# Pacing the last head's sums, splitting two weight sums ahead, and moving one norm step in a two-layer decoder trunk

## The chip, the cores and the metric

The kernel runs on one core of a Trainium2 chip. The metric is the device time of one execution in microseconds (us), taken as the median of three runs. The engines are named as the profile names them: PE is TensorE's matmuls, PEld its weight loads, DVE is VectorE, ACT is ScalarE, POOL is GpSimd and SP is SyncE, which here only issues DMAs. "SPq" and "POOLq" are the DMA queues of SP and POOL.

## The reference

The reference is two layers on x of shape (1024 positions, 1024 channels), all in fp32:

```python
for i in range(2):
    if i == 0:  y = mlstm_branch(x)       # x @ w_in, conv, 4 heads of a chunked matrix memory, group norm, gates, @ w_out
    else:       y = shortconv_branch(x)   # x @ w_in (1024x8192), gated 3-tap conv, silu gate, @ w_out (2048x1024)
    x = layer_norm(ALPHA * x + y, ln_g[i], ln_b[i])
    gate = sigmoid(x @ ple_gate_w[i])
    x = x + gate * (p[i] @ ple_w[i])
```

## The kernel before, in words

All activations lie channels first: a tile is 128 channels by 512 positions ("a slot"; 98 slots rotate), and h = 0 or 1 is the half of the positions. One fp32 product is made of three matmuls (`three`, L101 to L106): each operand is split into a high part that is rounded to fp32r (a cast on ACT, L91) and a low part, the rest (a subtraction on DVE, L94; L128 and L129 for a negated operand). L104 is high by high, L105 low weights by high, L106 high by low: "PE waits for L94" means that a low part was late. The big products use Strassen-like sums, seven products in place of eight, so weights and moving tiles are first added to each other. DVE makes such sums of moving tiles (`combined`, L118); DMAs that add in memory make those of weights (`add_on`, L135, on POOL's queue).

The program is written out in order by Python. A scheduler keeps that order mostly, engine by engine; generators that are stepped between products decide where the small work stands. The stages, by their part names: "in" (first projection), "at" (the four heads; items of one 128-position key block each), "outa" (projection out of layer 0), "ga" (norm and gate of layer 0), "b" (first projection of layer 1 with its convolution), "outb" (projection out of layer 1), "gb" (norm and gate of layer 1, output).

What the change touches:

- `norm` (L850 to L912) is the group norm after a head's half. For each of four channel tiles c it transposes on PE (L573), and DVE multiplies by the weight and the gate (L891) and adds the skip (L893). When four tiles of a pair are there, they are stored to DRAM (`store_plain`), and `store_sums` (L158) makes four sums on DVE (L118) and stores them on SP's queue (L152). For heads 0 to 2 that is done in the norm; for the last head the sums are deferred to `finish_cell` (L1369), which makes four at once in every second unit of outa from unit 9 on. The last head's h = 1 norm runs beside the first units of outa.
- `Out` (L198) runs a projection out as 56 units, each one weight tile and one moving tile, 12 matmuls. `load` fetches them about four units ahead by SP (L227), `prepare` splits both two units ahead. The weights of units s1 to s4 are sums that `weight_sums` (L171) made earlier and kept in DRAM (`wsdram`) as one fp32 tile each. Each of `outa` and `outb` is one `Out`.
- `layer_norm` (L1021) runs as a generator beside the matmuls. It makes the mean by matmul (L1017 with `mean`), subtracts (DVE L1036), squares (ACT L1038), adds the squares on POOL (L1010, L1012), and gets the variance (L1047). Then a diagonal tile is made (L1057), split, and multiplied by ones (`rs`, L1017 with `onesr`), so that 1/sigma stands in every partition. After it DVE multiplies eight tiles by `rs` (L1069) and ACT scales each (L1070). `NORM_WAITS[h]` says how many steps lie between these. In ga the gate of h = 1 needs those eight tiles; the gate's groups for h = 0 run meanwhile, each ending in a sigmoid (ACT L1186), a product and a sum on DVE (L1187, L1188) and splits for layer 1 (L91, L128, L1405).

Of the kernel before, what the change touches and what calls it, by code (L numbers as in the profile page):

```python
# [60 lines left out]
def trunk(ctx: ExitStack, tc: tile.TileContext, I, out: bass.AP):  # L61
# [48 lines left out]
    ydram = dr.tile([2, 7, 8, P, HALF], F32, name="ydram")  # L110
    wsdram = dr.tile([2, 4, 8, P, HALF], F32, name="wsdram")
    gwdram = dr.tile([2, 4, 7, 2, P, HALF], F32, name="gwdram")
# [45 lines left out]
    def store_sums(layer, kk, y11, y12, y21, y22):  # L158
        n3 = combined(y12, y22, ALU.subtract)
        t1 = combined(y12, y11, ALU.subtract)  # L160
        t2 = combined(y11, n3, ALU.subtract)
        n4 = combined(y21, t2, ALU.subtract)
        for what, y in (("t2", t2), ("t1", t1), ("n3", n3), ("n4", n4)):
            store(layer, kk, what, y)

    def store_moving(layer, kk, *ys):

        store_plain(layer, kk, *ys)
        store_sums(layer, kk, *ys)

    def weight_sums(layer, weights):  # L171

        rows = lambda k, i: weights[cols(k), cols(i, HALF)]
        store = lambda n, kk, t: nc.sync.dma_start(wsdram[layer, n, kk], t)
        s4 = None
        for kk in range(8):
            if s4 is not None:
                store(3, kk - 1, s4)
            s1, s2, s3, s4 = (slot() for _ in range(4))
            for t, src in ((s1, rows(2 * kk, 1)), (s2, rows(2 * kk, 0)), (s3, rows(2 * kk, 0)),  # L180
                           (s4, rows(2 * kk + 1, 0))):
                nc.sync.dma_start(t, src)
            yield
            add_on(s1, rows(2 * kk + 1, 1))
            add_on(s3, rows(2 * kk, 1))
            yield
            add_on(s2, s1)
            store(0, kk, s1)
            store(2, kk, s3)
            s1 = s3 = None  # L190
            yield
            add_on(s4, s2)
            store(1, kk, s2)
            s2 = None
            yield
        store(3, 7, s4)

    class Out:  # L198
# [8 lines left out]
        def __init__(self, layer, weights, residual):  # L207
            self.w, self.y, self.x, self.ready = {}, {}, {}, {}
            self.loads, self.loaded, self.prepared = [], 0, 0
            rows = lambda k, i: weights[cols(k), cols(i, HALF)]  # L210
            for what, kk in self.UNITS:
                if what in SUMS:
                    w = wsdram[layer, SUMS.index(what), kk]
                else:
                    w = rows(2 * kk + (what != "a11"), int(what == "a22"))
                m = MOVING[what]
                unit = [(self.w, (what, kk), w), (self.y, (m, kk), ydram[layer, STORED.index(m), kk])]
                for c, h, when in ((0, 0, ("a12", 4)), (0, 1, ("s2", 4)), (4, 1, ("s3", 4)), (4, 0, ("a22", 4))):
                    if (what, kk) == when:
                        unit += [(self.x, (c + t, h), residual(c + t, h)) for t in range(4)]  # L220
                self.loads.append(unit)

        def load(self, n):
            while self.loaded < min(n, len(self.UNITS)):
                for dst, key, src in self.loads[self.loaded]:
                    dst[key] = slot()
                    nc.sync.dma_start(dst[key], src)  # L227
# [519 lines left out]
    outa = Out(0, I["woa"], lambda k, h: I["xt"][cols(k), cols(h, HALF)])  # L747
    sums = weight_sums(0, I["woa"])

# [100 lines left out]
    def norm(hd, h, num, pacc, mv):  # L850
# [101 lines left out]
    for i in range(len(cell.order)):  # L952
# [11 lines left out]
        if i > 40 and cell.order[i][1] in (2, 5):  # L964
            step(sums)
        if i >= last:
            planned(i - last - 8)
# [5 lines left out]
    for _ in range(LEADS):  # L973
        lead()
    side = iter(())
    for i, (hd, h, s) in enumerate(items):
# [13 lines left out]
        if s >= 4 * h:  # L990
            close(num, s - 4 * h, mv)
        for _ in range(2):
            step(side)
        if i % 2:
            step(sums)
        outa.load((i - len(items) + 10) // 2)
        outa.prepare((i - len(items) + 6) // 2)
        if s == 4 * h + 3:
            drain(side)
            side = norm(hd, h, num, state.pop((hd, h))[1], mv)  # L1000
    last_norm = side
    drain(sums)
# [16 lines left out]

    NORM_WAITS = ((1, 3, 8, 2, 3), (1, 2, 2, 1, 1))  # L1020

    def layer_norm(layer, h, r, total, x, made, order):
        def waits(n):
            return range(NORM_WAITS[h][n])

# [28 lines left out]
        for _ in waits(3):  # L1054
            yield
        diag = slot()
        nc.vector.tensor_tensor(out=diag.rearrange("p (j c) -> p j c", c=P),  # L1057
                                in0=ident.unsqueeze(1).to_broadcast([P, 4, P]),
                                in1=rt.unsqueeze(2).to_broadcast([P, 4, P]), op=ALU.mult)
        parts = split(diag, "act", "dve")  # L1060
        del diag
# [307 lines left out]
    def finish_cell(u):  # L1369
        for _ in range(2):  # L1370
            step(last_norm)
        if u >= 9 and u % 2 and deferred:
            store_sums(*deferred.pop(0))

# [109 lines left out]
    outb = Out(1, I["wob"], lambda k, h: x2dram[k, h])  # L1484
    sums, gate_sums = weight_sums(1, I["wob"]), gate_weights(1, I["wgb"])
    for i, (g, n) in enumerate(mixer.order):
# [8 lines left out]
        if n in GATE_STEPS and 2 < g:  # L1495
            step(gate_sums)
    drain(sums)
    drain(gate_sums)
# [122 lines left out]
```

## Time and profile before

| | |
|---|---|
| median of 3 runs | 1932.34 us (1931.35 to 1933.34) |
| the profiled execution's own time | 1929.58 us |
| its span | 1927.8 us |
| PE busy | 1897.8 us (98%) |
| DVE, ACT, POOL busy | 1466.4, 939.5, 286.6 us |
| granted PE clock over the span | 0.998 of full speed |

The profiled execution's time lies 1.8 us above its span, which is what lies around the first and last instruction. Read the stages by time: "in" to 380 us, "at" to 778, "outa" to 928, "ga" to 1060, "b" to 1670, "outb" to 1813, "gb" to the end. Matmuls are pipelined: at full clock one of 128x512 starts every 0.227 us, though each row shows 0.39 us for it.

### The profile page before, as it was taken

To read this page: it belongs to the slowest core of one execution; us is meant where nothing else is said; L and a number is where in the kernel's file an instruction comes from. 1 tells how busy PE (TensorE), PEld (TensorE's weight loads), DVE (VectorE), ACT (ScalarE), POOL (GpSimd) and SP (SyncE) were. 2 spreads that over 40 slices of the span, in tenths; PEclk is the share of its full clock that TensorE was granted. 3 is DMA by queue.
4 is the path that set the end of the run, shared out by engine and by line. 5 is a ranking of instruction groups with operands and counts; after the bars stand their busy time and mean duration, and the time that the engine had idled before them with its cause. 6 is when DMAs were issued, how large, how long until landed. Compare 5 with 4: busy or idle time off the path is not lost. (4 is left out here: it accounts for less than half of the span.)

```text
span 1927.8 us, 25984 instructions
## 1 busy us (share of the span) xinstructions
PE 1897.8 (98%) x8654; PEld 1561.4 (81%) x8654; DVE 1466.4 (76%) x2528; ACT 939.5 (49%) x1741; POOL 286.6 (15%) x344
## 2 busy tenths in 40 slices
PE   8999999999999999999999999999999999999998
PEld 6778888888888888787878788888888888888787
DVE  7888888777777778668867787877787876846857
ACT  7555554546655544554664333333333333444553
POOL 1112332222001000034401000000000000022420
PEclk9999999999999999999999999999999999999999
DMA  8247767686556575896136535545545345597335
GB/s 252 92 153 226 240 214 232 202 242 247 163 204 213 184 269 184 311 341 189 52 131 164 145 132 155 186 147 166 174 160 179 130 141 172 201 334 240 121 115 191
DMA packets 192791, 365.95 MB, mean 190 GB/s; under 512 B 22256, under 2 KB 26640, under 8 KB 192656
## 3 DMA queue, kind: packets, MB, share of 16 engines
q1 hardware_dynamic: 164400, 293.49, 44.8%
q0 software_dynamic: 28256, 70.80, 14.2%
q8 instruction: 68, 1.11, 0.2%
q14 instruction: 67, 0.55, 0.1%
HBM read 235.21 MB, written 111.17 MB: 180 GB/s over the span
## 5 line engine op out<-in xcount | busy, mean ns | idle before, releaser
L104 PE MATMUL Pb<-ga,b 128*128 128x512 f32 x852 | 331.6, 389 | 0.7 <-ACT b L91 0.7
L105 PE MATMUL Pb<-ga,b 128*128 128x512 f32 x852 | 331.4, 389 | 0.0
L106 PE MATMUL Pb<-ga,b 128*128 128x512 f32 x852 | 327.3, 389 | 0.4 <-DVE b L94 0.3
L91 ACT CAST b<-b 128x512 fp32r<-128x512 f32 x249 | 144.6, 617 | 160.4 <-DVE b L118 160.2
L104 PE MATMUL Pin<-in,in 128*128 128x512 f32 x488 | 191.0, 391 | 2.4 <-ACT in L91 1.3
L105 PE MATMUL Pin<-in,in 128*128 128x512 f32 x488 | 190.0, 389 | 0.0
L106 PE MATMUL Pin<-in,in 128*128 128x512 f32 x488 | 189.0, 391 | 0.0
L106 PEld LDWEIGHTS Pb<-ga,b 128*128 128x128 f32 x852 | 159.9, 188 | 34.4 <-DVE b L94 1.3
L104 PEld LDWEIGHTS Pb<-ga,b 128*128 128x128 f32 x852 | 159.9, 188 | 34.4 <-ACT b L91 1.4
L105 PEld LDWEIGHTS Pb<-ga,b 128*128 128x128 f32 x852 | 159.9, 188 | 33.2
L94 DVE TENSOR_TENSOR b<-b,b 128x512 fp32r<-128x512 f32 x249 | 166.2, 684 | 21.8 <-ACT b L91 20.3
L91 ACT CAST in<-in 128x512 fp32r<-128x512 f32 x175 | 105.2, 613 | 90.7 <-DVE in L118 78.4
L94 DVE TENSOR_TENSOR in<-in,in 128x512 fp32r<-128x512 f32 x175 | 118.4, 686 | 24.1 <-ACT in L91 23.4
L123 ACT ACTIVATE b<-Pb 128x512 f32<-128x512 f32 x96 | 57.5, 599 | 135.9 <-PE Pb L106 135.8
L104 PE MATMUL Pat<-at,at 128*128 128x512 f32 (+3 forms) x297 | 112.1, 378 | 0.9 <-ACT at L91 0.9
L118 DVE TENSOR_TENSOR b<-b,b 128x512 f32<-128x512 f32 x167 | 110.6, 685 | 0.8
L104 PEld LDWEIGHTS Pin<-in,in 128*128 128x128 f32 x488 | 91.6, 188 | 23.5 <-ACT in L123 2.1
L106 PE MATMUL Pat<-at,at 128*128 128x512 f32 (+3 forms) x297 | 109.4, 371 | 1.2 <-DVE at L833 1.2
L105 PE MATMUL Pat<-at,at 128*128 128x512 f32 (+3 forms) x297 | 109.8, 370 | 0.0
L106 PEld LDWEIGHTS Pin<-in,in 128*128 128x128 f32 x488 | 91.6, 188 | 20.8 <-DVE in L94 1.7
L105 PEld LDWEIGHTS Pin<-in,in 128*128 128x128 f32 x488 | 91.6, 188 | 18.7
L94 DVE TENSOR_TENSOR outa<-outa,outa 128x512 fp32r<-128x512 f32 x108 | 78.9, 785 | 24.9 <-ACT outa L91 24.6
(424 smaller groups left out, 4244.2 us busy)
## 6 DMA issues: line engine op xcount, KB each, us to landing
b<-wb SPq DMA_DIRECT2D x122, 256.0 KB, 4.0
in<-wa SPq DMA_DIRECT2D x86, 256.0 KB, 4.2
xcdram<-in POOLq DMA_DIRECT2D x56, 256.0 KB, 4.5
ydram<-b SPq DMA_DIRECT2D x56, 256.0 KB, 2.1
gwdram<-b SPq DMA_DIRECT2D x56, 256.0 KB, 2.2
gb<-gwdram SPq DMA_DIRECT2D x56, 256.0 KB, 3.7
outa<-ydram SPq DMA_DIRECT2D x52, 256.0 KB, 5.7
outb<-ydram SPq DMA_DIRECT2D x49, 256.0 KB, 5.4
```

The costliest lines, as they stand in the source:

```text
L91: nc.scalar.copy(hi, src)
L94: (nc.vector if lo_on == "dve" else nc.gpsimd).tensor_tensor(out=lo, in0=src, in1=hi.bitcast(F32), op=ALU.subtract)
L104: mm(acc, lh, rh, start=first, stop=False, skip_group_check=onto)
L105: mm(acc, lh, rl, start=False, stop=False, skip_group_check=onto)
L106: mm(acc, ll, rh, start=False, stop=last, skip_group_check=onto)
L118: nc.vector.tensor_tensor(out=d, in0=a, in1=b, op=op)
L123: nc.scalar.activation(t, src, AF.Copy, scale=scale)
```

## The change

Three groups of edits. First, `store_sums` becomes a generator with one sum and one store per step: heads 0 to 2 step it in the norm, and for the last head `finish_cell` makes one step in every unit. The norm's steps per item become `NORM_STEPS`, and the last head's h = 1 norm waits one step in place of two in two places and takes one step a unit in outa. Second, for layer 1 the weight sums s1 and s4 are split into their two parts in stage b (`split_sum`, one per group at product 1) and kept in DRAM as two tiles; outb then loads two finished parts and splits only the moving tile. Third, `NORM_WAITS` is given per layer and half: in layer 0, h = 1, the last wait (between diagonal and `rs`) is 2 in place of 1; in layer 1, h = 0, the third (between squares and variance) is 9 in place of 8; the diagonal and its split get the scheduler's high priority.

```diff
+NORM_STEPS = (2, 2, 1)
+NORMS_AT_ONCE = 0
+SPLIT_STEPS = (1, 4)
...
+    TWO_PARTS = ((), ("s1", "s4"))
...
     def store_sums(layer, kk, y11, y12, y21, y22):
         n3 = combined(y12, y22, ALU.subtract)
+        yield
         t1 = combined(y12, y11, ALU.subtract)
+        store(layer, kk, "n3", n3)
+        del y12, y22
+        yield
         t2 = combined(y11, n3, ALU.subtract)
+        store(layer, kk, "t1", t1)
+        del y11, n3, t1
+        yield
         n4 = combined(y21, t2, ALU.subtract)
-        for what, y in (("t2", t2), ("t1", t1), ("n3", n3), ("n4", n4)):
-            store(layer, kk, what, y)
+        store(layer, kk, "t2", t2)
+        del y21, t2
+        yield
+        store(layer, kk, "n4", n4)
...
+        def split_one():
+            if ended:
+                n, kk, t = ended.pop(0)
+                store(n, kk, *(x.bitcast(F32) for x in split(t, "act", "dve")))
...
+                for n, t in ((0, s1), (3, s4)):
+                    if SUMS[n] in TWO_PARTS[layer]:
+                        ended.append((n, kk, t))
+                    else:
+                        store(n, kk, t)
...
+                if what in TWO_PARTS[layer]:
+                    unit = [(self.w, (what, kk, i), wsdram[layer, SUMS.index(what), kk, i]) for i in range(2)]
...
-                left = split(self.w.pop((what, kk)), "act", "dve")
+                if (what, kk, 0) in self.w:
+                    left = self.w.pop((what, kk, 0)), self.w.pop((what, kk, 1))
+                else:
+                    left = split(self.w.pop((what, kk)), "act", "dve")
...
-        for _ in range(RESTS):
+        for _ in range(1 if hd == HEADS - 1 and h else RESTS):
             yield
...
-        for _ in range(SETTLE):
+        for _ in range(1 if hd == HEADS - 1 and h else SETTLE):
             yield
...
-                    deferred.append((0, ct // 2, *ys))
+                    deferred.append(store_sums(0, ct // 2, *ys))
                 else:
                     yield
-                    store_sums(0, ct // 2, *ys)
+                    yield from store_sums(0, ct // 2, *ys)
...
-    NORM_WAITS = ((1, 3, 8, 2, 3), (1, 2, 2, 1, 1))
+    NORM_WAITS = {(0, 0): (1, 3, 8, 2, 3), (0, 1): (1, 2, 2, 1, 2), (1, 0): (1, 3, 9, 2, 3), (1, 1): (1, 2, 2, 1, 1)}
...
-        parts = split(diag, "act", "dve")
+        with tc.high_priority():
+            nc.vector.tensor_tensor(out=diag.rearrange("p (j c) -> p j c", c=P),
+                                    in0=ident.unsqueeze(1).to_broadcast([P, 4, P]),
+                                    in1=rt.unsqueeze(2).to_broadcast([P, 4, P]), op=ALU.mult)
+            parts = split(diag, "act", "dve")
...
-        for _ in range(2):
-            step(last_norm)
-        if u >= 9 and u % 2 and deferred:
-            store_sums(*deferred.pop(0))
+        for _ in range(NORM_STEPS[2]):
+            norm_step()
+        if u >= 9 and deferred and not step(deferred[0]):
+            deferred.pop(0)
...
+        if n == SPLIT_STEPS[0]:
+            split_sum()
```

Line numbers shift: L91, L94, L129 of before are L94, L97, L132 of the changed kernel, L104 to L106 are L107 to L109, L573 is L611, L891 and L893 are L929 and L931, L1017 is L1064, L1036 is L1083, L1069 and L1070 are L1117 and L1118, L1111 is L1159, and L1186 is L1234.

**Start of outa, DVE.** Before, from the third channel tile's product (L891 on outa_..._8071) on; outa_..._8091 and outa_..._8095 are low parts of a unit's weight and moving tile:

```order
1178 L891 SCALAR_TENSOR_TENSOR outa_1845_8071<-Pouta_1856_8113,cpack_157,outa_1845_8071 128x512
1179 L893 TENSOR_TENSOR outa_1845_8071<-outa_1845_8071,outa_1846_8072 128x512
1180 L891 SCALAR_TENSOR_TENSOR outa_1848_8082<-Pouta_1863_8144,cpack_157,outa_1848_8082 128x512
1181 L94 TENSOR_TENSOR outa_1853_8091<-outa_1828_8008,outa_1852_8090 128x512
1182 L893 TENSOR_TENSOR outa_1848_8082<-outa_1848_8082,outa_1849_8083 128x512
1183 L129 SCALAR_TENSOR_TENSOR outa_1855_8095<-outa_1829_8010,outa_1854_8094 128x512
```

The same place of the changed kernel:

```order
1178 L929 SCALAR_TENSOR_TENSOR outa_1845_8071<-Pouta_1868_8161,cpack_157,outa_1845_8071 128x512
1179 L97 TENSOR_TENSOR outa_1850_8080<-outa_1828_8008,outa_1849_8079 128x512
1180 L931 TENSOR_TENSOR outa_1845_8071<-outa_1845_8071,outa_1846_8072 128x512
1181 L132 SCALAR_TENSOR_TENSOR outa_1852_8084<-outa_1829_8010,outa_1851_8083 128x512
1182 L929 SCALAR_TENSOR_TENSOR outa_1854_8106<-Pouta_1875_8192,cpack_157,outa_1854_8106 128x512
```

The unit's low parts moved ahead of the fourth tile's product. On PE the last transpose of the third tile moved the other way, from row 3486, ahead of a unit's matmuls, to row 3498, behind them:

```order
3496 L108 MATMUL Pouta_1837_8023<-outa_1843_8049,outa_1840_8044 128x512
3497 L109 MATMUL Pouta_1837_8023<-outa_1842_8048,outa_1841_8045 128x512
3498 L611 MATMUL Pouta_1868_8161<-cpack_157,at_1816_7975 128x128
3499 L611 MATMUL Pouta_1875_8192<-cpack_157,at_1808_7955 128x128
3500 L611 MATMUL Pouta_1875_8192<-cpack_157,at_1816_7975 128x128
```

So row 1178 on DVE waits for PE's row 3498. The deferred sums (L118, now L121) moved too: two blocks of four on DVE (rows 1196 to 1199 and 1204 to 1207) became single rows between splits (1196, 1199, 1202, 1205 and 1218, 1221, 1224, 1227). Their stores, and SP's loads for outa's units behind them, now read:

```order
456 L156 DMA ydram_73<-outa_1952_8482 128x512
457 L262 DMA outa_1964_8519<-wsdram_74 128x512
458 L262 DMA outa_1965_8521<-ydram_73 128x512
459 L156 DMA ydram_73<-outa_1963_8516 128x512
460 L262 DMA outa_1971_8546<-wsdram_74 128x512
461 L262 DMA outa_1972_8548<-ydram_73 128x512
462 L156 DMA ydram_73<-outa_1970_8543 128x512
463 L262 DMA outa_1978_8573<-wsdram_74 128x512
464 L156 DMA ydram_73<-outa_1977_8570 128x512
465 L262 DMA outa_1979_8575<-ydram_73 128x512
```

Before, the four stores of this pair stood at SP's rows 440 to 443, twelve tile loads earlier.

**The norm of h = 1 in ga, PE.** Before, the two matmuls of `rs` stand right behind a gate group of 24 (Pga_..._9947):

```order
4275 L105 MATMUL Pga_2342_9947<-outa_2257_9607,ga_2322_9877 128x512
4276 L106 MATMUL Pga_2342_9947<-outa_2256_9606,ga_2323_9878 128x512
4277 L1017 MATMUL Pga_2348_9982<-ga_2344_9962,onesr_194 128x512
4278 L1017 MATMUL Pga_2348_9982<-ga_2345_9963,onesr_194 128x512
4279 L104 MATMUL Pga_2361_10014<-outa_2228_9494,ga_2325_9883 128x512
```

In the changed kernel they stand at the end of the next group:

```order
4298 L107 MATMUL Pga_2358_10005<-outa_2256_9606,ga_2336_9935 128x512
4299 L1064 MATMUL Pga_2359_10018<-ga_2344_9962,onesr_194 128x512
4300 L108 MATMUL Pga_2358_10005<-outa_2257_9607,ga_2336_9935 128x512
4301 L109 MATMUL Pga_2358_10005<-outa_2256_9606,ga_2337_9936 128x512
4302 L1064 MATMUL Pga_2359_10018<-ga_2345_9963,onesr_194 128x512
```

The second one moved from row 4278 to row 4302. On ACT the changed kernel then has these rows between the first scaled tile (L1118) and the cast of a weight that the group after next needs (ga_..._10056); the PE row that needs it is 4339 in both kernels:

```order
989 L1118 ACTIVATE outa_1958_8494<-outa_1958_8494,cpack_157 128x512
990 L94 CAST ga_2355_9999<-ga_2341_9945 128x512
991 L1118 ACTIVATE outa_2015_8714<-outa_2015_8714,cpack_157 128x512
992 L94 CAST ga_2360_10023<-outa_1955_8488 128x512
993 L1118 ACTIVATE outa_2016_8716<-outa_2016_8716,cpack_157 128x512
994 L1118 ACTIVATE outa_2017_8718<-outa_2017_8718,cpack_157 128x512
995 L94 CAST ga_2362_10041<-outa_1956_8490 128x512
996 L1118 ACTIVATE outa_2018_8720<-outa_2018_8720,cpack_157 128x512
997 L1234 ACTIVATE ga_2364_10045<-Pga_2358_10005 128x512
998 L94 CAST ga_2365_10050<-ga_2364_10045 128x512
999 L1453 ACTIVATE ga_2367_10054<-ga_2364_10045 128x512
1000 L94 CAST ga_2368_10056<-ga_2354_9997 128x512
```

Rows 983 to 988, ahead of these, are three more L1118 and three casts of that size. So eight L1118 and six others stand ahead of the sigmoid in row 997; before, the order was the same kind, with the sigmoid in row 998.

**End of outb, DVE.** Before, between the last subtractions of the norm's mean (L1036) and the next evictions (L1111), the low parts of units' weights (outb_..._17230, 17270, 17302, 17326) alternate with those of moving tiles:

```order
2365 L94 TENSOR_TENSOR outb_3980_17234<-outb_3954_17160,outb_3979_17233 128x512
2366 L1036 TENSOR_TENSOR outb_3906_16960<-outb_3906_16960,Poutb_3971_17214 128x512
2367 L94 TENSOR_TENSOR outb_3988_17270<-outb_3965_17190,outb_3987_17269 128x512
2368 L94 TENSOR_TENSOR outb_3990_17274<-outb_3966_17192,outb_3989_17273 128x512
2369 L94 TENSOR_TENSOR outb_3996_17302<-outb_3975_17225,outb_3995_17301 128x512
2370 L94 TENSOR_TENSOR outb_3998_17306<-outb_3976_17227,outb_3997_17305 128x512
2371 L94 TENSOR_TENSOR outb_4002_17326<-outb_3985_17265,outb_4001_17325 128x512
2372 L94 TENSOR_TENSOR outb_4004_17330<-outb_3986_17267,outb_4003_17329 128x512
```

Now only those of moving tiles are left:

```order
2376 L97 TENSOR_TENSOR outb_4009_17308<-outb_3987_17242,outb_4008_17307 128x512
2377 L1083 TENSOR_TENSOR outb_3938_17040<-outb_3938_17040,Poutb_4001_17290 128x512
2378 L97 TENSOR_TENSOR outb_4018_17346<-outb_3998_17272,outb_4017_17345 128x512
2379 L97 TENSOR_TENSOR outb_4025_17376<-outb_4007_17305,outb_4024_17375 128x512
2380 L97 TENSOR_TENSOR outb_4030_17398<-outb_4016_17343,outb_4029_17397 128x512
```

Half of the splits of this stretch are gone. Over both units s1 and s4 it is 16 L94 and 16 casts less in outb and as many more in b; SP has 16 more stores in b and 16 more loads in outb, and no other engine has more or fewer rows. The `rs` of this norm moved seven PE rows back.

## Rows read from the trace of the kernel before

**Rows 1.** The page's busy times, with share of the span and instructions.

```profile
PE 1897.8 (98%) x8654; PEld 1561.4 (81%) x8654; DVE 1466.4 (76%) x2528; ACT 939.5 (49%) x1741; POOL 286.6 (15%) x344
```

**Rows 2.** Windows ga and b: length, PE, PEld, DVE, ACT, POOL busy; clock, DMA, GB/s.

```profile
960.00:1060.00 100.00, 97.34 (x424) 79.58 (x422) 71.75 (x111) 56.59 (x104) 11.11 (x11) 0.98 0.48 143
1060.00:1570.00 510.00, 508.86 (x2242) 420.44 (x2242) 395.71 (x664) 183.90 (x327) 24.33 (x28) 1.00 0.51 159
```

**Rows 3.** PE's waits by releaser: total us, times, longest us.

```profile
PE Pat L789 <- DVE at L891: 3.7, 2, 2.2
PE Pin L104 <- ACT in L91: 3.3, 2, 2.0
PE Pga L1017 <- ACT ga L91: 2.4, 1, 2.4
...
PE Pouta L105 <- DVE outa L129: 1.7, 1, 1.7
```

**Rows 4.** Timeline at outa's start: start, us, engine, line, tiles, count, idle before.

```profile
785.15 0.38 PE L573 MATMUL Pouta<-cpack,at 128*128 128x128 f32 x2
...
787.47 0.68 DVE L129 SCALAR_TENSOR_TENSOR outa<-outa,outa 128x512 fp32r<-128x512 f32 x1
...
788.21 0.51 PE L105 MATMUL Pouta<-outa,outa 128*128 128x512 f32 x1 [1.75 <-DVE outa L129]
```

**Rows 5.** Timeline of PE at the norm of h = 1 in ga.

```profile
970.01 0.39 PE L106 MATMUL Pga<-outa,ga 128*128 128x512 f32 x1
972.84 0.51 PE L1017 MATMUL Pga<-ga,onesr 128*128 128x512 f32 x1 [2.44 <-ACT ga L91]
973.57 0.50 PE L1017 MATMUL Pga<-ga,onesr 128*128 128x512 f32 x1 [0.22 <-DVE ga L94]
...
989.14 0.39 PE L104 MATMUL Pga<-outa,ga 128*128 128x512 f32 x1
```

**Rows 6.** Windows behind three idle times of PE: columns as in rows 2.

```profile
31.80:36.00 4.20, 4.13 (x11) 2.97 (x12) 4.20 (x8) 4.20 (x9) 1.42 (x3) 0.59 0.43 138
...
558.60:562.00 3.40, 3.40 (x23) 3.12 (x24) 3.40 (x8) 1.86 (x5) 0.00 (x0) 1.00 0.40 150
...
974.50:978.00 3.50, 3.50 (x10) 2.71 (x9) 3.50 (x7) 3.17 (x6) 0.00 (x0) 0.51 0.00 0
```

**Rows 7.** Timelines of DVE and ACT behind the `rs` of rows 5.

```profile
974.11 3.08 DVE L1069 TENSOR_TENSOR outa<-outa,Pga 128x512 f32<-128x512 f32 x5
...
977.96 2.92 ACT L1070 ACTIVATE outa<-outa,cpack 128x512 f32<-128x512 f32 x4
...
984.61 0.59 ACT L1186 ACTIVATE ga<-Pga 128x512 f32<-128x512 f32 x1
...
988.09 1.13 ACT L91 CAST ga<-ga 128x512 fp32r<-128x512 f32 x2
```

**Rows 8.** Timelines of DVE and POOL at the end of outb.

```profile
1785.96 8.59 DVE L94 TENSOR_TENSOR outb<-outb,outb 128x512 fp32r<-128x512 f32 x6
...
1783.11 10.29 POOL L1012 TENSOR_TENSOR outb<-outb,outb 128x512 f32<-128x512 f32 x6 [0.32 <-ACT outb L1038]
```

**Rows 9.** Windows over the end of outb: columns as in rows 2.

```profile
1740.00:1760.00 20.00, 20.00 (x90) 16.52 (x89) 11.05 (x19) 11.13 (x23) 3.50 (x4) 1.00 0.93 261
1760.00:1780.00 20.00, 19.77 (x87) 15.84 (x86) 11.65 (x14) 2.71 (x6) 6.45 (x4) 1.00 0.70 210
1780.00:1800.00 20.00, 18.84 (x83) 14.36 (x82) 19.18 (x25) 11.76 (x22) 12.01 (x8) 1.00 0.22 70
1800.00:1820.00 20.00, 19.53 (x86) 15.85 (x85) 18.27 (x27) 14.34 (x25) 5.32 (x4) 1.00 0.63 194
```

**Rows 10.** A moving tile in outa: SP's issue, median to landing, matmul using it.

```profile
820.15 0.32 SPq L227 DMA_DIRECT2D outa<-ydram  x1
...
outa<-ydram SPq DMA_DIRECT2D x52, 256.0 KB, 5.7
...
838.72 0.39 PE L105 MATMUL Pouta<-outa,outa 128*128 128x512 f32 x1
```

More of the change, by code (lines that the diff above doesn't have):

```diff
@@ L110, in trunk @@
     ydram = dr.tile([2, 7, 8, P, HALF], F32, name="ydram")
-    wsdram = dr.tile([2, 4, 8, P, HALF], F32, name="wsdram")
+    wsdram = dr.tile([2, 4, 8, 2, P, HALF], F32, name="wsdram")
     gwdram = dr.tile([2, 4, 7, 2, P, HALF], F32, name="gwdram")
@@ L166, in store_moving @@
+        yield
+        store(layer, kk, "n4", n4)
     def store_moving(layer, kk, *ys):
         store_plain(layer, kk, *ys)
-        store_sums(layer, kk, *ys)
+        drain(store_sums(layer, kk, *ys))
     def weight_sums(layer, weights):
         rows = lambda k, i: weights[cols(k), cols(i, HALF)]
[L174 to L182, printed above, removed]
-            yield
[L184 to L195, printed above, removed]
@@ L196, in weight_sums, with store, steps @@
-        store(3, 7, s4)
+        ended = []
+        def store(n, kk, *ts):
+            for i, t in enumerate(ts):
+                nc.sync.dma_start(wsdram[layer, n, kk, i], t)
+        def split_one():
+            if ended:
+                n, kk, t = ended.pop(0)
+                store(n, kk, *(x.bitcast(F32) for x in split(t, "act", "dve")))
+        def steps():
+            for kk in range(8):
+                s1, s2, s3, s4 = (slot() for _ in range(4))
+                for t, src in ((s1, rows(2 * kk, 1)), (s2, rows(2 * kk, 0)), (s3, rows(2 * kk, 0)),
+                               (s4, rows(2 * kk + 1, 0))):
+                    nc.sync.dma_start(t, src)
+                yield
+                add_on(s1, rows(2 * kk + 1, 1))
+                add_on(s3, rows(2 * kk, 1))
+                yield
+                add_on(s2, s1)
+                store(2, kk, s3)
+                s3 = None
+                yield
+                add_on(s4, s2)
+                store(1, kk, s2)
+                s2 = None
+                yield
+                for n, t in ((0, s1), (3, s4)):
[3 more added lines that the diff above has]
+                        store(n, kk, t)
+                del t
+                del s1, s4
+            yield
+            while ended:
+                split_one()
+                yield
@@ L198, in trunk @@
+        return steps(), split_one
     class Out:
@@ L225, in load @@
                 for dst, key, src in self.loads[self.loaded]:
-                    dst[key] = slot()
-                    nc.sync.dma_start(dst[key], src)
+                    two = dst is self.w and len(key) > 2
+                    dst[key] = slot(F32R if two else F32)
+                    nc.sync.dma_start(dst[key].bitcast(F32) if two else dst[key], src)
                 self.loaded += 1
@@ L965, in trunk @@
             step(sums)
+        if i > 40 and cell.order[i][1] == SPLIT_STEPS[1]:
+            split_sum()
         if i >= last:
@@ L974, in trunk, with norm_step @@
         lead()
-    side = iter(())
+    norms = []
+    def norm_step():
+        while norms and next(norms[0], norms) is norms:
+            norms.pop(0)
     for i, (hd, h, s) in enumerate(items):
@@ L991, in trunk @@
             close(num, s - 4 * h, mv)
-        for _ in range(2):
-            step(side)
+        for _ in range(NORM_STEPS[h]):
+            norm_step()
         if i % 2:
             step(sums)
+        elif h:
+            split_sum()
         outa.load((i - len(items) + 10) // 2)
@@ L998, in trunk @@
         if s == 4 * h + 3:
-            drain(side)
-            side = norm(hd, h, num, state.pop((hd, h))[1], mv)
-    last_norm = side
+            while len(norms) > NORMS_AT_ONCE:
+                norm_step()
+            norms.append(norm(hd, h, num, state.pop((hd, h))[1], mv))
     drain(sums)
@@ L1369, in finish_cell @@
     def finish_cell(u):
-        for _ in range(2):
-            step(last_norm)
-        if u >= 9 and u % 2 and deferred:
-            store_sums(*deferred.pop(0))
+        for _ in range(NORM_STEPS[2]):
+            norm_step()
+        if u >= 9 and deferred and not step(deferred[0]):
+            deferred.pop(0)
     pw, pt = [], ([], [])
@@ L1496, in trunk @@
             step(gate_sums)
+        if n == SPLIT_STEPS[0]:
+            split_sum()
     drain(sums)
```

19 lines of the change are left out of this document (8 added, 11 removed).

## The prediction

> **What bounds the kernel now.** I read the page's busy times first: PE works 1897.8 us of a span of 1927.8 [rows 1]. Everything that any edit can give is therefore among the 30 us in which PE stands idle, plus whatever it runs at less than full clock. Next come the windows by stage: the long stage b has 1.1 us of idle in 510, the stage with the first norm and gate loses 2.7 us in 100 and has a mean clock of 0.98 [rows 2]. Then PE's waits by releaser say which of these the change can reach [rows 3]: one wait of 2.4 us for a cast ahead of `rs` in ga, one of 1.7 us for a low part at the start of outa. The waits of the attention stage (L789 on L891) and of the first stage (L104 on a cast) are out of its reach, since PE's, DVE's and ACT's orders of heads 0 to 2 and of the first stage do not change. A third place is the end of outb: 1.16 us idle in 1780 to 1800, 0.47 in 1800 to 1820 and 0.23 before [rows 9]. From the same windows comes the pace: 2242 matmuls in 508.86 us is 0.227 us each.
>
> **A, the start of outa.** PE waits 1.75 us at 788.21 for the low part that DVE starts at 787.47 [rows 4]. In the new order that low part has two DVE operations fewer ahead of it, 2 x 0.68 = 1.35 us if nothing else bound it. But the third tile's product, ahead of it, now waits for a transpose that stands behind twelve matmuls, beside the two transposes that start at 785.15 and take 0.38 us together [rows 4]. From there: product to about 786.1, then the low part of the weight and the sum at about 0.6 us each, then ours at 787.3 in place of 787.47. Gain 0.2 us; I take it with bounds 0 and 1.35. The wait moves little; its name stays L129 (now L132).
>
> **B, the norm in ga.** Two things sit here. PE is idle for 2.44 and 0.22 us ahead of the two `rs` matmuls [rows 5], and then the granted clock is 0.51 from 974.5 to 978.0, the lower of the two levels (1.2 of 2.4 GHz) [rows 6]. The loss is 3.50 x 0.49 = 1.7 us. Together they explain nearly all of this: from PE's row 4276 (970.01) to row 4339 (989.14 [rows 5]) are 63 matmuls, 63 x 0.227 = 14.3 us, but it took 19.1. So 4.8 us are lost, and that is the most B can give. In the new order `rs` stands 24 rows later, its diagonal is long ready, and both waits go.
>
> What is late next is the chain that `rs` releases. Its second matmul would start at 970.01 + 26 x 0.227 = 975.9 in place of 973.57 [rows 5], 2.3 us later. The first of DVE's eight products followed 0.54 us behind (974.11 [rows 7]), so now at 976.4, and ACT's first scaling 0.7 us on, at 977.1. ACT has eight scalings of 0.73 us (2.92 us for four [rows 7]; some run 0.71) and six casts of 0.52 ahead of the sigmoid: about 8.8 us, so the sigmoid starts at 985.9, where it started at 984.61 before [rows 7]. From sigmoid to the weight's cast that PE's row 4339 needs, before took 988.09 + 0.57 - 984.61 = 4.05 us [rows 7], with DVE's product and sum and two ACT operations in it; the same steps stand in the new order. The cast is then ready at 990.0. PE, without waits until then, would want it at 984.3. It will first stop for casts of the group before (row 4315, wanted at 978.9, and that cast stands behind two scalings in ACT's order: about 980.1; its low part about 0.5 later), and then, for row 4339, some 3.5 us in one piece. Row 4339 comes at 990.0 in place of 989.14: B costs 0.85 us. ACT was full there before as well, so the old idle time and slow clock had cost almost nothing at this row: the cast was ready only 0.45 us before it was used. Behind it the next operands are due at nearly the same pace, and I see no later place where the stage makes the time good.
>
> To this comes the clock. Three idle times of PE are to be compared: behind one of 2.0 us (the first wait of the first stage) the clock was 0.59 over 4.2 us, behind one of 2.2 us (L789) it stayed at 1.00, and behind the one of 2.44 us it was 0.51 [rows 3, 6]. The new piece of 3.5 us is longer than any of these, so I take a drop: 1.7 us of matmul time, which this time falls behind the last late cast, where nothing absorbs it. The Trainium skill, "TensorE: Matmul & The Clock Gate", section "What's actually happening", says that the throttled state is the default, released by activity, and that the observation runs free of the kernel's own start. By that rule a drop is partly a matter of phase, and the trace agrees as far as it goes (a shorter idle dropped it, a longer one did not); B would be 0.85 us or 2.55. I give the drop 7 in 10. B is +2.55 us; bounds -4.8 (the chain is not last after all) and +3.
>
> **C, the end of outb.** DVE's six low parts from 1785.96 take 8.59 us, 1.43 each in place of 0.68, while POOL adds the squares, six adds in 10.29 us [rows 8]. Three of the six, and 16 over both units, are now made in b. PE's idle there is 1.16 + 0.47 + 0.23 = 1.86 us [rows 9]; 0.47 of it is the wait before `rs`, which moves seven rows (1.6 us) back with a third wait of 9. The other low parts still run under POOL's adds, three at 1.43 us, against units of 12 x 0.227 = 2.7 us; so they keep up. I take 1.5 us of gain, with bounds 0.5 and 1.86. The Trainium skill, "SBUF — State Buffer", section "SBUF: two separate sides", says that VectorE and GpSimd take turns on a shared read path, one waiting for the whole of the other's instruction. By that rule a single low part under a POOL add can still be held for an add (10.29 / 6 = 1.7 us, our row), and the gain would be nearer 0.5 us.
>
> **D, what C moves elsewhere, and the rest.** Sixteen casts and sixteen low parts go into b, one pair to a group. DVE is 78% busy there (395.71 of 510), ACT 36%, PE idle 1.1 us [rows 2]: cost nothing, hidden behind 0.227 x 84 = 19 us of matmuls per group; without cover each pair would cost up to 0.68 us, 11 us in all. Sixteen stores in b and sixteen loads in outb are 256 KB each. In outb a unit then loads three tiles. The DMA share is 0.93 in 1740 to 1760, 0.70 and 0.22 after [rows 9], so 37 us of the 60 are taken. At 261 GB/s, the rate of the fullest window, 16 loads are 4.19 MB or 16 us; they fit in the 23 us left, and these loads are needed up to 1820. Cost nothing, up to 2 us if the tiles come late. The stores of the last head's sums are a rival, below. Heads 0 to 2: the engines that compute keep their order; the stores only move within SP's queue.
>
> **Sum.** -0.2 + 0.85 + 1.7 - 1.5 + 0 = +0.85 us on the profiled 1929.58 us, which is 1.8 above its span; on the median of 1932.34 that is 1933.2. The median stands 2.8 us above the profiled execution, so the change is smaller than what separates two executions.
>
> **Rivals.**
> 1. The chain is late but the clock holds: -0.85 us, 1931.5. For it: the idle of 2.2 us after which the clock stayed. Against it: 3.5 us in one piece.
> 2. B gives its full 4.8 us, because DVE or ACT run the chain in time (an order that keeps pace, or a late cast already made). With A and C -6.5 us: 1925.8. For it: PE's waits in the row of releasers name only the diagonal's cast. Against it: ACT's order, in which every row up to the sigmoid is busy.
> 3. C does not do what it says: the low parts of the moving tiles alone keep PE waiting, or the three loads of a unit arrive as late as the splits did. Then 1.5 us are missing: 1934.7.
> 4. Slower: SP's queue in outa. The second pair's four stores now stand one by one between loads (rows 456 to 465), and each waits for a DVE sum that comes behind other splits; the loads behind them wait with it. The last of them was issued at 820.15 and its unit wanted at 838.72, with 5.7 us to landing as the median [rows 10]. If SP is held for the four sums until about 826 to 830, landing is near 834, the split near 835.3, and 3 us are spare. It decides once SP is held 3 us longer than that: each us more is a us of idle, and with 3 us of it and a clock drop of 1.7 the sum is +0.85 + 4.7, 1937.9.
>
> **How the numbers follow.** Chances: my forecast 0.50; rival 1 0.20; rival 2 0.12; rival 3 0.08; rival 4 0.10. The forecast's own range is 1931 to 1935.5, by B's and C's bounds with the chain holding. The range given, 1928.0 to 1936.0, takes in rivals 1 and 3 and leaves out rival 2 and most of rival 4, 2 in 10. About 0.2%, 3.9 us, is what a measurement of this kernel can tell from no change: faster than 1928.5 is rival 2 and a little of rival 1, 0.14; slower than 1936.2 is rival 4, 0.10; the rest, 0.76, lies between.
>
> **What would show it.** Right: in ga no wait at `rs` (L1064), but waits of PE on ACT L94 or DVE L97 some 10 us behind it, the longest about 3.5 us, and a stretch of clock near 0.5 behind that; the matmul of row 4339 about 19 to 20 us behind row 4276. In outa a wait of about 1.5 us on L132; at the end of outb no wait on L97 and DVE under 80% in the 20 us where it was 96%. Wrong: ga without a wait over 1 us (rival 2); waits in outb on L97 or on `wsdram` (rival 3); PE waiting in outa for a landing near 838 (rival 4); or PE idle in b, which would say that the extra splits there do not hide.

## The result and the profile after

The changed kernel takes 1936.84 us in the median (1934.94 to 1942.5, 8 runs) against 1931.86 before (8 runs), a ratio of 1.0028 with a 95% interval of 1.0016 to 1.0040. Timed again in a later set it was 1935.14, ratio 1.0019 (1.0011 to 1.0028). By these two ratios it is slower by 5.4 and 3.7 us; I had forecast 1933.2 and given "slower by more than 3.9 us" one chance in ten.

The page of the changed kernel's profiled execution (span 1933.7 us) has PE busy 2.7 us longer for the same number of instructions as in [rows 1]. That is what matmuls at half clock look like there: of the profiles in the table below, the two with a single fall of the clock have PE busy for 1896.1 and 1896.4 us, the two with four falls for 1900.0 and 1900.5.

```profile
PE 1900.5 (98%) x8654; PEld 1564.7 (81%) x8654; DVE 1465.8 (76%) x2528; ACT 940.5 (49%) x1741; POOL 284.6 (15%) x344
```

PE's waits by releaser in the changed kernel (total us, times, longest), to hold against [rows 3]:

```profile
PE Pga L107 <- ACT ga L94: 4.2, 2, 3.1
...
PE Pouta L108 <- DVE outa L97: 2.1, 3, 1.1
PE Poutb L1094 <- POOL outb L1059: 2.1, 1, 2.1
PE Pouta L108 <- DVE outa L132: 1.5, 1, 1.5
...
PE Pouta L107 <- ACT outa L94: 1.2, 1, 1.2
```

The wait at `rs` in ga is gone, and two in its stead sum to 4.2 us, the longer one 3.1. The one on L132 is 0.25 shorter. Two are new: 2.1 us for POOL's last addition in outb (L1094, the variance; L1047 before), and 1.2 us for a cast in outa.

The same kernel's windows behind its longer idle times (columns as in [rows 2]):

```profile
558.00:562.00 4.00, 3.64 (x18) 3.47 (x19) 4.00 (x9) 1.38 (x4) 0.00 (x0) 0.65 0.50 189
632.00:638.00 6.00, 4.92 (x23) 4.39 (x24) 5.47 (x10) 1.96 (x5) 0.00 (x0) 0.72 0.41 153
...
994.10:999.00 4.90, 4.84 (x21) 3.93 (x22) 4.14 (x7) 3.07 (x7) 0.00 (x0) 1.00 0.34 115
...
1797.00:1801.00 4.00, 4.00 (x13) 3.20 (x14) 0.00 (x0) 0.00 (x0) 0.00 (x0) 0.66 0.00 0
```

The kernel before has full clock in the first two of these stretches:

```profile
558.00:562.00 4.00, 3.49 (x23) 3.21 (x24) 4.00 (x9) 1.86 (x5) 0.00 (x0) 1.00 0.49 188
632.00:638.00 6.00, 6.00 (x36) 5.27 (x35) 5.34 (x11) 2.95 (x8) 0.00 (x0) 1.00 0.39 133
```

So in this profile the clock fell behind two old waits of the attention stage, where it had not before, and behind the new wait in outb, but not behind the 3.1 us in ga.

To see where time goes I take, from PE's timeline, the start of the first matmul that writes each stage's tiles (for outa the first one of L104, now L107). In the kernel before these are 492.84, 771.39, 927.98, 1048.98 and 1663.24 us, and the last matmul starts at 1921.89. The differences are the times of the stages. "Falls" are the stages in which the granted clock fell. Stage b takes 613.9 to 615.1 us in all of them.

| kernel | at | outa | ga | outb + gb | falls | ratio to before |
|---|---|---|---|---|---|---|
| before | 278.55 | 156.59 | 121.00 | 258.65 | in, ga | |
| before again | 277.65 | 156.52 | 121.45 | 258.73 | in | |
| changed | 281.95 | 157.68 | 121.69 | 259.54 | in, at twice, outb | 1.0028 |
| changed again | 281.01 | 157.34 | 123.50 | 257.76 | at, ga | 1.0019 |
| variance kept | 277.57 | 158.63 | 124.26 | 256.11 | in, ga | 1.0004 |
| sums in fours | 277.63 | 156.18 | 121.73 | 259.42 | outb | 1.0015 |
| ga wait 1 | 280.47 | 158.43 | 121.21 | 259.50 | in, at, ga, outb | 1.0011 |
| variance kept, fours | 280.01 | 156.18 | 123.91 | 256.07 | in, at, ga | 0.9990 |
| the same, ga wait 1 | 278.40 | 156.21 | 122.02 | 256.09 | in, ga | 0.9983 |
| the same, diagonal first | 280.03 | 156.18 | 124.65 | 256.05 | at, ga | 0.9994 |
| paced on POOL's queue | 280.11 | 156.17 | 121.23 | 256.42 | in, at, ga | 0.9975 |
| old group-norm waits | 278.35 | 156.55 | 121.54 | 256.03 | in, ga | 0.9986 |

### The profile page after: what moved, and what is told of

It is laid out like the page before. It is cut to its first block, busy times and chain, and to the rows that moved or that the text cites. A ratio compares the mean times of both kernels' runs of the same rounds, so it can differ in the third digit from the quotient of the medians.

```text
span 1933.7 us, 26052 instructions
## 1 busy us (share of the span) xinstructions
PE 1900.5 (98%) x8654; PEld 1564.7 (81%) x8654; DVE 1465.8 (76%) x2528; ACT 940.5 (49%) x1741; POOL 284.6 (15%) x344
## 4 chain that ended last, share of the span: by engine, by line
PE 86%; DVE 5%; DMA 5%; ACT 2%; issue 2%; POOL 1%; SPq 0%; DVEq 0%; ACTq 0%; POOLq 0%
PE Pb L109 10%; PE Pb L108 10%; PE Pb L107 10%; PE Pin L107 7%; PE Pin L109 7%; PE Pin L108 7%; PE Pat L107 3%; PE Pat L108 3%; PE Pat L109 3%; PE Poutb L108 2%; PE Poutb L109 2%; PE Poutb L107 2%; PE Pga L107 2%; PE Pga L109 2%; PE Pga L108 2%
## 5 line engine op out<-in xcount | busy, mean ns | idle before, releaser
L107 PE MATMUL Pb<-ga,b 128*128 128x512 f32 x852 | 331.6, 389 | 0.7 <-ACT b L94 0.7
L109 PE MATMUL Pb<-ga,b 128*128 128x512 f32 x852 | 327.3, 389 | 0.3 <-DVE b L97 0.3
L94 ACT CAST b<-b 128x512 fp32r<-128x512 f32 x265 | 152.3, 616 | 161.0 <-DVE b L121 158.6
L107 PE MATMUL Pin<-in,in 128*128 128x512 f32 x488 | 191.0, 391 | 2.4 <-ACT in L94 1.3
L97 DVE TENSOR_TENSOR b<-b,b 128x512 fp32r<-128x512 f32 x265 | 176.4, 685 | 17.2 <-ACT b L94 15.7
L109 PE MATMUL Pin<-in,in 128*128 128x512 f32 x488 | 189.0, 390 | 0.0
L109 PEld LDWEIGHTS Pb<-ga,b 128*128 128x128 f32 x852 | 160.0, 188 | 34.3 <-DVE b L97 1.2
L107 PEld LDWEIGHTS Pb<-ga,b 128*128 128x128 f32 x852 | 160.0, 188 | 34.2 <-ACT b L94 1.2
L94 ACT CAST in<-in 128x512 fp32r<-128x512 f32 x175 | 105.3, 613 | 90.5 <-DVE in L121 86.2
L97 DVE TENSOR_TENSOR in<-in,in 128x512 fp32r<-128x512 f32 x175 | 118.5, 686 | 23.9 <-ACT in L94 21.9
L107 PE MATMUL Pat<-at,at 128*128 128x512 f32 (+3 forms) x297 | 113.0, 381 | 0.9 <-ACT at L94 0.9
L121 DVE TENSOR_TENSOR b<-b,b 128x512 f32<-128x512 f32 x167 | 110.7, 686 | 0.8
L109 PE MATMUL Pat<-at,at 128*128 128x512 f32 (+3 forms) x297 | 109.9, 373 | 1.2 <-DVE at L871 1.2
L107 PEld LDWEIGHTS Pin<-in,in 128*128 128x128 f32 x488 | 91.6, 188 | 23.5 <-ACT in L126 2.1
L109 PEld LDWEIGHTS Pin<-in,in 128*128 128x128 f32 x488 | 91.6, 188 | 20.6 <-DVE in L97 1.7
L97 DVE TENSOR_TENSOR outa<-outa,outa 128x512 fp32r<-128x512 f32 x108 | 82.4, 803 | 24.3 <-ACT outa L94 23.9
```

The source lines that it names most:

```text
L94: nc.scalar.copy(hi, src)
L97: (nc.vector if lo_on == "dve" else nc.gpsimd).tensor_tensor(out=lo, in0=src, in1=hi.bitcast(F32), op=ALU.subtract)
L107: mm(acc, lh, rh, start=first, stop=False, skip_group_check=onto)
L109: mm(acc, ll, rh, start=False, stop=last, skip_group_check=onto)
L121: nc.vector.tensor_tensor(out=d, in0=a, in1=b, op=op)
```

## The experiments

Every ratio is to the kernel before, timed in the same set; the second profile of the kernel before has one time and no ratio. "Theory 1" is that the loss lies at places of its own (outb, outa, ga), with the clock lost behind waits by chance; the rival is that the clock lost in the attention stage belongs to the change.

**The variance kept in its place.** PE's order in outb differs from before in one thing that the part on the change does not show. The four variance matmuls, eight instructions in the trace, stood together; in the changed kernel the scheduler has lifted two of them over 24 other matmuls. Before:

```profile
1797.47 0.95 PE L1047 MATMUL Poutb<-ones,outb 128*128 128x4 f32 x8
```

The changed kernel:

```profile
1796.49 0.61 PE L1094 MATMUL Poutb<-ones,outb 128*128 128x4 f32 x4 [2.08 <-POOL outb L1059]
...
1804.15 0.50 PE L1094 MATMUL Poutb<-ones,outb 128*128 128x4 f32 x4
```

The edit holds all four where the program writes them:

```diff
-            mm(var[:, cols(j, 4)], squares[1][:, cols(j)], ones[:, :4], start=True, stop=True)
+            tc.keep_in_program_order(mm(var[:, cols(j, 4)], squares[1][:, cols(j)], ones[:, :4], start=True, stop=True))
```

> The changed kernel, with the four variance matmuls of outb's norm kept where the program writes them (after a third wait of 9), in place of two of them standing 32 rows earlier. Theory 1 (the loss lies at named places: 2.1 us of waiting for POOL's last addition and about 1.6 us of half clock behind it in outb, 1.4 us in outa, 0.3 us in ga, and the rest is clock lost behind old waits of the attention stage, by chance): the wait of PE on POOL L1059 is gone, the clock stays at 1.00 from 1790 to 1806, and the time falls by 2.5 to 4 us from 1936.8 to 1933 to 1934.5, ratio to before 1.0005 to 1.0015. Rival (the loss is the attention stage's clock, brought by the new order of stores there, and outb's wait only takes what the missing splits gave): the time falls by under 1 us, ratio 1.002 to 1.003, since a wait comes back at the next low part.

Measured: 1931.6 us, ratio 1.0004 (0.9995 to 1.0012), a little more of a gain than theory 1 expected. In the changed kernel those two matmuls await the end of POOL's additions:

```profile
1787.00 9.43 POOL L1059 TENSOR_TENSOR outb<-outb,outb 128x512 f32<-128x512 f32 x6
```

They end at 1796.43. PE was there at 1794.41 and stands until then. In the kernel before they had ended at 1793.40 [rows 8], 4.1 us ahead of PE. Counted from the stage's first matmul (1663.24, now 1668.17), PE comes to the variance 8.0 us sooner, and 24 x 0.227 = 5.4 of these are the lift; POOL ends 1.9 us sooner. With the variance kept, the windows of this stretch are at full clock:

```profile
1785.00:1795.00 10.00, 10.00 (x46) 8.29 (x45) 8.36 (x9) 7.46 (x15) 9.41 (x7) 1.00 0.55 192
1795.00:1805.00 10.00, 9.70 (x46) 7.61 (x45) 6.81 (x9) 0.00 (x0) 6.87 (x5) 1.00 0.41 134
```

and PE's waits in outb come down to one:

```profile
PE Poutb L108 <- DVE outb L132: 0.2, 1, 0.2
```

Theory 1 holds here, and the rival for this place is out: outb and gb take 2.6 us less than before. The changed kernel took 0.9 more in its first profile, with a fall of the clock, and 0.9 less in its second, without one.

**The sums in fours again.**

```diff
-        if u >= 9 and deferred and not step(deferred[0]):
-            deferred.pop(0)
+        if u >= 9 and u % 2 and deferred:
+            drain(deferred.pop(0))
```

> The changed kernel, with the last head's deferred sums made four at a time in every second unit again, as before; all else of the change stays. Theory 1: SP is no longer held from 815 to 839 us, the 1.2 us wait of PE near 861 on an ACT cast is gone, the time falls by 1 to 1.6 us to about 1935.5, ratio about 1.002. Rival: outa's late cast is made up later, no change, ratio 1.0028.

Measured: 1934.33 us, ratio 1.0015 (1.0006 to 1.0025). outa takes 156.2 us, where the four profiles with paced sums on SP's queue have 157.3 to 158.6. The changed kernel's SP and, below, what came of it:

```profile
812.04 3.17 SPq L262 DMA_DIRECT2D outa<-xt  x4
827.04 0.33 SPq L156 DMA_DIRECT2D ydram<-outa  x1
...
834.65 0.32 SPq L156 DMA_DIRECT2D ydram<-outa  x1
837.50 0.32 SPq L262 DMA_DIRECT2D outa<-ydram  x1
...
859.49 1.66 ACT L94 CAST outa<-outa 128x512 fp32r<-128x512 f32 x3 [3.62 <-DMA outa<-plew]
...
861.21 0.50 PE L107 MATMUL Pouta<-outa,outa 128*128 128x512 f32 x1 [1.20 <-ACT outa L94]
```

SP issues nothing from 815 to 827, then a store and up to two loads at a time until 837.5 (820.15 for the same tile in [rows 10]). PE doesn't miss that unit. It misses one 20 us on: the DMA engines are full by then (busy share 1.07 from 855 to 862), a cast of an embedding weight waits on ACT for a late landing, and behind it in ACT's order stands the cast that PE wants. In three other profiles with this pacing the same wait is 0.85, 1.71 and 1.85 us; with sums in fours there is none.

**ga's wait back to 1.** `NORM_WAITS[0, 1]` ends in 1 in place of 2; the diagonal keeps its priority.

> The changed kernel, with the last wait of layer 0, h = 1, at 1 again, so that the two matmuls of rs stand where they stood before. Theory 1 (chain of norm bound by ACT, the same end whichever wait is set): PE waits 2.4 us at rs again, no wait over 1 us later in ga, row 4339 about 0.3 to 0.6 us sooner against the entry of ga, and the time within 1 us of 1936.8, ratio 1.0022 to 1.0030. Rival (the chain starts later and this loses 2 us and more): ratio under 1.0018.

Measured: 1934.28 us, ratio 1.0011 (1.0002 to 1.0020). By the ratio that is the rival, which had named less than 1.0018. The profiles show both. Without a fall of the clock wait 2 costs 0.5 us (121.7 against 121.2), as theory 1 had it. With wait 1 the clock fell in ga and cost nothing there (as in [rows 5, 6]); with wait 2 it costs 2 us and more when it falls, which is the rival's size.

**The kernel before, profiled again.**

> The kernel before, unchanged, profiled again: shows whether the clock falls behind the old waits of the attention stage (558 and 631 us) in this kernel too. Theory 1: the set of waits behind which the clock is near half differs from the first profile's (one in the first stage and one in ga), since it is chance; the span differs from 1927.8 by 1.7 us for each. Rival (these drops come with the changed order of stores): again no drop at 558 and 631, span within 1 us of 1927.8.

Measured: span 1927.1 us, 1928.91 in the one run. The clock fell in the first stage alone, not in ga behind a wait of 2.45 us at the same place. The span shrank by 0.7 and not by 1.7, and ga took 121.45 in place of 121.00: ga's fall had cost next to nothing. In ga it is chance, then. At 558 and 632 the clock held again, as the rival said; one profile can't decide on the attention stage.

**The changed kernel, profiled again.**

> The changed kernel, unchanged, profiled again beside the others of this set. Theory 1 (three waits of its own, and clock lost by chance behind them and behind old ones): the ratio is 1.0028 within 0.001; PE waits about 2.1 us for POOL at the variance in outb with half clock behind it again, outa from its first to ga's first matmul is 157.5 to 159 us (156.5 before), ga to b 121.7 without a drop of the clock or 124 with one. The attention stage is 277.6 us, or 1.7 more for each drop there, and another number of drops than in the first profile. Rival (the drops at 559 and 634 us belong to the change): the attention stage takes 282 us again.

Measured: 1935.14 us, ratio 1.0019. This time the clock held at 558 and fell at 632, and behind the 3.05 us in ga, and held in outb behind the same 2.08 us. The attention stage took 281.0 us with its one fall, between theory 1's 279.3 and the rival's 282, and the wait ahead of the fall was 2.45 us (1.44 before):

```profile
558.00:562.00 4.00, 3.44 (x23) 3.18 (x24) 4.00 (x9) 1.86 (x5) 0.00 (x0) 1.00 0.50 192
632.00:638.00 6.00, 5.68 (x26) 5.30 (x27) 5.07 (x10) 2.07 (x5) 0.00 (x0) 0.72 0.36 131
...
992.90:998.00 5.10, 5.05 (x15) 3.92 (x16) 4.35 (x7) 3.26 (x8) 0.00 (x0) 0.67 0.34 125
```

**Variance kept and sums in fours.** Both edits above on the changed kernel.

> The changed kernel with the variance matmuls kept in place and the last head's sums in fours; what is left of the change is the later rs in ga, the two-part sums and the shorter waits of the last group norm. Theory 1: outa 156.2 us, outb and gb together 256.1 (258.6 before), ga 121.7 or 124.2: against before -0.4, -2.5 and +0.3 to +2.8, in sum -2.6 to -0.1; ratio 0.9987 to 1.0000. Rival (two undone edits are not additive, as a late stage absorbs): ratio 1.0004 as with the variance alone.

Measured: 1929.61 us, ratio 0.9990 (0.9981 to 0.9999). The terms add, and the 1.0004 that the rival had named lies outside the interval.

**The same with ga's wait at 1.**

> As the one with variance kept and sums in fours, and rs of ga back behind the first group (last wait 1). Theory 1: ga takes 121.0 to 121.5 us whether or not the clock falls there, since PE's slow matmuls lie where PE would wait for ACT anyway; ratio 0.9980 to 0.9990, 0.3 to 1.5 us under the one with wait 2. Rival (wait 2 is as good, its 3 us in one piece drop the clock no oftener): the same time within 0.3 us.

Measured: 1928.16 us, ratio 0.9983 (0.9975 to 0.9992), 1.45 us under the one with wait 2, though the two intervals overlap. Theory 1's size for ga (121.0 to 121.5) was a little short of the measured 122.02.

**The diagonal first.** `NORM_WAITS[0, 1] = (1, 2, 2, 0, 2)`, to bring `rs` sooner, not later.

> As the one with variance kept and sums in fours, with the waits around ga's diagonal 0 and 2 in place of 1 and 2: the diagonal is made five rows sooner on DVE, and rs stands behind the first group as before. Theory 1 (the chain behind rs bounds ga, so rs must come sooner, not later): the wait at rs falls from 2.4 us to under 1, the chain starts 2 us or more sooner, and ga takes 119 to 120 us in place of 121; ratio 0.997 to 0.999. Rival (the h = 0 results that now stand behind the diagonal on DVE are late instead): ga 121 or more, ratio as with wait 1.

Measured: 1931.25 us, ratio 0.9994 (0.9986 to 1.0003): the rival. `rs` no longer waits, yet ga is 124.65. The waits are those of the changed kernel, one group sooner in PE's order:

```profile
PE Pga L107 <- ACT ga L94: 4.7, 2, 3.0
PE Pga L109 <- DVE ga L97: 0.8, 2, 0.5
```

So an earlier `rs` alone does not help; what PE waits for are ACT's casts of the next weights, and they stand behind eight scalings and a sigmoid. ACT of the changed kernel, ahead of PE's 3.07 us wait:

```profile
989.67 0.81 ACT L1118 ACTIVATE outa<-outa,cpack 128x512 f32<-128x512 f32 x1
990.39 0.57 ACT L1234 ACTIVATE ga<-Pga 128x512 f32<-128x512 f32 x1
992.45 0.62 ACT L94 CAST ga<-ga 128x512 fp32r<-128x512 f32 x1 [1.48 <-DVE ga L1236]
992.97 0.62 ACT L1453 ACTIVATE ga<-ga 128x512 f32<-128x512 f32 x1
993.50 1.12 ACT L94 CAST ga<-ga 128x512 fp32r<-128x512 f32 x2
...
994.16 0.50 PE L107 MATMUL Pga<-outa,ga 128*128 128x512 f32 x1 [3.07 <-ACT ga L94]
```

The cast from 993.50 needs nothing that is late: the last weights loaded ahead of it had landed by 986.1. It stands behind operations that wait for the sigmoid, and the sigmoid stands behind the scalings.

**Paced sums, their stores on POOL's queue.** On the changed kernel with the variance kept and ga's wait at 1:

```diff
-    def store_sums(layer, kk, y11, y12, y21, y22):
+    def store_sums(layer, kk, y11, y12, y21, y22, queue=nc.sync):
...
-                    deferred.append(store_sums(0, ct // 2, *ys))
+                    deferred.append(store_sums(0, ct // 2, *ys, queue=nc.gpsimd))
```

> The changed kernel with the variance matmuls kept and rs of ga back at wait 1; the last head's sums are paced one a unit as in the change, but their stores are issued on POOL's queue in place of SP's. Theory 1 (what costs in outa is that SP's loads stand behind stores that wait for paced sums): SP's issues between 815 and 839 us are no longer held, no wait over 1 us of PE near 858 to 861, outa takes 156.2 us or less (157.3 to 158.6 with the stores on SP, 156.2 with sums in fours), ratio 0.998 to 0.999. Rival (the sums' place among DVE's splits costs, whoever stores them): outa 157.3 us or more, ratio about 0.9995.

Measured: 1927.69 us, ratio 0.9975 (0.9966 to 0.9984), the fastest of all. outa is 156.17, and PE has no wait near 860. But half of what I expected is wrong: SP is held all the same, for one load of a stored sum,

```profile
SPq L262 <- DMA ydram<-outa: 26.8, 2, 23.3
```

for 23.3 us in one piece. What changed is the end: from here on

```profile
832.41 0.32 SPq L262 DMA_DIRECT2D outa<-ydram  x1
```

the loads go out one behind the other, where the changed kernel was held again and again until 837.5. Counted from outa's first matmul (772.71 here, 774.81 there), the next loads of `xt` begin at 65.5 us here and at 68.5 there. That those 3 us are what reached PE at 861 is my reading; no run moves them alone. The stages give some 2.7 us of this kernel's gain (outa -0.4, outb and gb -2.3), its ratio 4.8 with 3.1 as the least of its interval; what the rest is stays open.

**The old waits of the last group norm.** On the kernel with ratio 0.9983, `RESTS`, `SETTLE` and two steps a unit as before.

> The fastest kernel so far (variance kept, sums in fours, rs of ga at wait 1) with the last group norm's waits and steps as before. Theory 1: PE waits 1.75 us at the start of outa in place of 1.50, outa 156.5 us in place of 156.2, and outb and gb stay at 256.1: nearly all of what that kernel gains on before is the two-part sums; ratio 0.9985 within 0.0008. Rival (half of the gain is in the shorter waits): ratio 0.9992 or more.

Measured: 1929.86 us, ratio 0.9986 (0.9977 to 0.9995). outa is 156.55, the wait on L132 1.8 again. The shorter waits give the 0.3 us that the stage shows; the time alone couldn't tell it.

## Why the prediction was wrong

**The sum's term for outb failed, and it came out with the other sign.** The prediction read the stretch from DVE: fewer low parts, so no waits, -1.5 us. That mechanism was right and even too small: with the variance kept, outb and gb take 256.1 us against 258.7, -2.6, with PE's waits there down from 2.1 to 0.6 us. The failed step is the sentence that `rs` moves seven rows back, taken as all that moves on PE there; the part on the change, which says that no engine but SP has more or fewer rows, misses the same thing. The group of four variance matmuls was cut in two, its first half 24 matmuls sooner. In before POOL's additions had ended 4.1 us ahead of PE [rows 8]; now PE came 2.08 us too soon. The four profiles with this order give 257.8 to 259.5, mean 259.05, so the term is +0.4 in place of -1.5. The wait alone makes it 257.8 (-0.9), and the clock fell behind it in three of the four (259.4 to 259.5, +0.8).

**A was right in its own size; the pacing of the sums, which the sum put at nothing, was not nothing.** The wait on L132 went from 1.75 to 1.50 (0.2 forecast). The fourth rival had the mechanism of the pacing and gave it 0.10: it named the stores that hold SP. It looked for the harm at the unit whose load is held, at 838. SP held that load longer than the rival's 830, but the tile was there 2.7 us behind its issue (837.50, its cast from 840.22) and not 5.7, and PE has no wait there. The harm came 20 us later, through full DMA engines and ACT's order. Its price was 4.7 us, 1.7 of them a fall of the clock; measured are 0.8 to 2.1 in outa, without a fall (157.34 to 158.63 against 156.55).

**B held.** The forecast was +0.85 us without and +2.55 with a fall of the clock, at 7 in 10. Measured: 121.7 against 121.0 to 121.45 (+0.2 to +0.7) without, 123.5 to 124.65 (+2.1 to +3.6) with, and the fall in four of six profiles with such a wait of 3 us. Row 4339 comes 19.63 us behind row 4276 in all five profiles with wait 2 and the diagonal in its old place, against 19.13 in before: +0.50, where the chain gave +0.85. That this row is set by ACT's chain was right. The experiment with the diagonal first adds that an earlier `rs` does not help, as the casts stand behind the sigmoid. Rival 2, the full 4.8 us, was out.

**D held**: b takes 614 to 615 us in every profile, the extra splits hide, and outb's extra loads make no wait.

**The sum.** From the table, against the means of before's two profiles: outa +1.5 (mean of the four profiles that pace the sums with the stores on SP, 158.0, less 156.55), ga +1.8 (mean of the five with wait 2 and the diagonal in its old place, 123.0, less 121.2), outb and gb +0.4, together +3.7 us. The second measurement's ratio says +3.7, the first one's +5.4, and its interval reaches down to +3.1. Against the +0.85 forecast, outb is 1.9 us worse and outa 1.7, and B came out 0.75 better, as the clock did not fall each time.

**What stays open.** In the attention stage the clock fell in none of two profiles of before and in six of ten of the kernels with the new order of stores. One fall there goes with 280.0 to 281.0 us, none with 277.6 to 278.6. Whether this order makes falls likelier can't be told from so few profiles, but the granted clock of all timed executions bounds it. A fall of 1.7 us takes 0.0009 off an execution's mean clock. Averaged over 8 to 33 executions, that mean is 0.9976 to 0.9979 for before in three sets, 0.9965 to 0.9972 in the four timings with the variance cut in two, and 0.9975 to 0.9982 in the six kernels that keep it together, which have the same new order of stores. So the cut group goes with about one fall more in each execution, and the order of stores with none that shows. The times agree: the last kernel of the table has that order too, and its ratio of 0.9986 (-2.7 us, 1.7 to either side) is what outb and gb alone give (-2.6). Not known is why PE's wait near 632 was 1.8 to 2.5 us in the three profiles in which the clock fell behind it, and at most 1.6 in the nine others.

## What to carry to other kernels

Compare the orders row by row on the engine that bounds, not only on the engine that the edit names: a group of four small matmuls on PE, cut in two and half of it lifted, cost 2.9 us here (259.05 against 256.1) and made a loss of that stage's gain. For each row that moves forward, ask how long its operand was ready before: POOL's sum had 4.1 us to spare, and the lift took 5.4. And a queue that issues in order passes one late store on to every load behind it, with the harm where the spare time runs out, not where the store stands.

## What the runs showed of the hardware

The same idle time of PE does or doesn't bring the clock down, from one execution to the next of one kernel: 2.44 us at `rs` in before did, 2.45 in its second profile did not; 3.07 us in the changed kernel did not, 3.05 in its second profile did. A longer idle was no surer: behind some 3.05 us in ga the clock fell in four of six profiles, behind 2.08 us in outb in three of four. A fall cost 1.7 us in outb, where PE is the bound behind it (257.77 without, 259.4 to 259.5 with), and about nothing in ga behind the wait at `rs`, where PE would stand waiting anyway (121.00 with, 121.45 without). So the wait of 2.08 us in outb cost 1.7 us without a fall (257.77 against 256.1) and 3.4 with one, which a single profile doesn't show. The spread of one kernel's times goes with the clock: of 27 executions of before in one set, those with a mean granted clock of 0.999, 0.998, 0.997 and 0.996 took 1929.65, 1931.03, 1932.67 and 1935.13 us on average.
